# Sparse attention with normalised queries, logits and extreme from one tensor_tensor_reduce, and token factors brought to channels by matmul with identity

## The chip, the cores and the metric

The kernel runs on one core of one Trainium2 chip. The core has TensorE (PE in the profile, its weight loads PEld), VectorE (DVE), ScalarE (ACT), GpSimd (POOL) and SyncE (SP), which issues most DMAs here. The metric is the device time of one execution in microseconds; lower is better.

## The reference, cut to what matters

One layer feeds a normalised input of 1024 tokens into five parallel branches (A, B, C, D, M), whose outputs are merged by gates and projected. The change is in branch C, sparse attention with 8 heads of 64 channels and one shared key and value head:

```python
q = rms_norm(q.reshape(Bsz, L, DSA_HEADS, DSA_HD), q_norm_g)
k = rms_norm(k, k_norm_g)
...
_, sel = lax.top_k(s_idx, top_k)
...
logits = jnp.einsum('bthd,btkd->bhtk', qb, k_sel).astype(f32) * DSA_HD ** -0.5
logits = logits - slopes[None, :, None, None] * dist[:, None]
logits = jnp.where(valid[:, None], logits, -jnp.inf)
p = jax.nn.softmax(logits, axis=-1).astype(v.dtype)
return jnp.einsum('bhtk,btkd->bthd', p, v_sel)
...
out * jax.nn.silu(gate)
```

`slopes` of head h is 2 to the power of -(h + 1). The kernel does not gather: it takes the logits of all keys up to the token's own tile, and a distance of 1e30 stands for a key that was not selected.

## The kernel before, in words

The kernel is written tile by tile. A planner at build time follows the source, allocates the buffers of each tag (`tag`, `bufs`) and fixes the order of every engine's queue: what stands earlier in the source goes first, later work that is ready fills the time that the planner's own clock shows as free, and `tc.issue_after(mark)` keeps work behind a marked instruction of the same engine. On the chip every queue then runs in that order.

Before branch C runs, `sc[j]` (128 tokens of tile j by 128(j+1) keys) holds, for each token and key, the distance to the key if it is selected and 1e30 otherwise. `keys_c` (L814) normalises the keys, puts them into two stacked operands `khh` and `kll`, and leaves the values by token in `vtok`. Both gains and the factor 64 ** -0.5 are in the keys.

Branch C works on 4 blocks b of two heads (`hf` 0 and 1, 64 channels each, on the two halves of the partitions). `prep(b)` (L840) loads the raw queries `cq` by channel, transposes them on TensorE (`pq`) to get the mean square of each token and head (`ms`), and has GpSimd raise it to the power of -0.5 (`rq`). The stacks `qst` are made from the raw queries by `stacks` (L312): a rounded copy on ScalarE, the remainder `qstl` on VectorE, and a DMA that puts the remainder on the other 64 partitions. `cf` is the slope divided by the token's query factor. The gate `sg` is loaded into the same buffer as the queries.

`attend(b, j)` (L862) handles 128 tokens against 128(j+1) keys, in three steps. In step one, TensorE makes the logits in PSUM (`lg`, at most 512 columns at a time, so j above 3 takes two pieces), VectorE subtracts `cf` times the distance, and takes the maximum of the row. ScalarE takes the exponential with `rq` as its scale and adds up the row in `sm`. VectorE inverts the sum, and GpSimd multiplies the identity by it into `dg`. In step two TensorE transposes the probabilities (`pT`), and ScalarE copies them to `pt`. In step three TensorE multiplies ones by `dg`, which spreads each token's factor over 64 channels, multiplies `vtok` by `pt`, and VectorE multiplies both products into the gate `sg`. `skew` starts a new unit in each round, and runs step two of the unit before and step three of the one before that. `prep(b + 1)` stands in front of unit 4 of block b.

The tiles of `sps` (logits, transposes, outputs and spreads) share 5 PSUM banks. Around the branch lie the merges, which project each finished branch: 16 groups of 12 matmuls of 128x512 (`proj`, in 3 banks of their own), each followed by a VectorE operation (`tgl`) and an addition on GpSimd (`mg`):

```python
branch("c", branch_c)
ckx.close()
merge(2, [None] * 2 + evenly(span["c"], 28))
merge(3)
```

Behind merge 3, `prep_out` loads the output weights (`wr`) and splits them on ScalarE and VectorE. They use the space that the score tiles `sc` leave.

Of the kernel before, what the change touches and what calls it, by code (L numbers as in the profile page):

```python
# [7 lines left out]
F32 = mybir.dt.float32  # L8
F32R = mybir.dt.float32r
I32 = mybir.dt.int32  # L10
AF = mybir.ActivationFunctionType
OP = mybir.AluOpType
AX = mybir.AxisListType
PSUM = bass.MemoryType.PSUM

P = 128
D = 1024
L = 1024
NT = L // P
# [6 lines left out]
MARK = -3.0e38  # L26
# [29 lines left out]
def mixer_body(ctx, tc, a, out):  # L56
    nc = tc.nc
    S, G = nc.scalar, nc.gpsimd
    V, T = Traced(nc.vector), Traced(nc.tensor)
# [17 lines left out]
    def sps(name):  # L77
        return gps(name, "s")
# [4 lines left out]
    ident = cst.tile([P, P], F32, name="ident")  # L83
    make_identity(nc, ident)
    nhalf = cst.tile([P, 64], F32, name="nhalf")
# [51 lines left out]
    HV = (slice(0, 512), slice(512, 1024))  # L137
# [66 lines left out]
    HF = (slice(0, 4), slice(4, 8))  # L204

    def r3(t, c=P):
        return t.rearrange("p (n c) -> p n c", c=c)
# [104 lines left out]
    def stacks(pool, ps, name, bufs, eng=V):  # L312

        t = [pool.tile([P, L], F32R, name=name, tag=name, bufs=bufs) for _ in range(2)]
        lo = pool.tile([P, L], F32R, name=name + "l", tag=name + "l", bufs=1)
        halves = ((slice(0, 64), slice(64, 128)), (slice(64, 128), slice(0, 64)))
        for hv, p in zip(HV, ps):
            for i, (r, o) in enumerate(halves):
                S.activation(t[i][r, hv], p[r], AF.Copy)
                eng.tensor_tensor(lo[r, hv], p[r], t[i][r, hv].bitcast(F32), OP.subtract)  # L320
        for i, (r, o) in enumerate(halves):
            nc.sync.dma_start(t[i][o].bitcast(F32), lo[r].bitcast(F32))
        return t

    def cuts(w):

        n = -(-w // 512)
        at = [-(-w * i // (n * P)) * P for i in range(n + 1)]
        return [(at[i], at[i + 1] - at[i]) for i in range(n)]

    def scores(name, q, j, kh, kl, c0, n):

        ps = sps(name)
        qj = q[:, j * P:(j + 1) * P]
        T.matmul(ps[:, :n], qj, kh[:, c0:c0 + n], start=True, stop=False)
        T.matmul(ps[:, :n], qj, kl[:, c0:c0 + n], start=False, stop=True)
        return ps
# [190 lines left out]
    def loaded(pool, nm, b, tag, bufs):  # L528

        t = pool.tile([P, L], F32, name=tag, tag=tag, bufs=bufs)  # L530
        nc.sync.dma_start(t, zd[nm][b])
        return t

    def halves(t):
        return [t[:, hv] for hv in HV]
# [280 lines left out]
    def keys_c(gp):  # L816
        kvr = loaded(gp, "c_k", 0, "uu", 2)
        kn2 = gp.tile([P, NT, 2, 64], F32, name="kn2", tag="uu", bufs=2)
        ksq = gp.tile([P, NT, 64], F32, name="ksq", tag="mx", bufs=2)
        kss = gp.tile([P, NT], F32, name="kss")  # L820
        kps = []
        for hf in HF:
            ps = tr4("kvT", lambda i: kvr[:, (hf.start + i) * P:(hf.start + i + 1) * P])
            kps.append(ps)
            S.activation(vtok[:, hf], r3(ps)[:, :, 64:128], AF.Copy)
            S.activation(ksq[:, hf], r3(ps)[:, :, 0:64], AF.Square)
        V.reduce_sum(kss, ksq, AX.X)
        rsqrt_into(kss, kss, NT, 1.0 / 64, EPS)
        for hf, ps in zip(HF, kps):
            V.tensor_tensor(ksq[:, hf], r3(ps)[:, :, 0:64], b3(kss[:, hf], 4, 64), OP.mult)  # L830
        for i in range(2):
            V.tensor_tensor(kn2[:, :, i, :], ksq, kgain[:, None, :].to_broadcast([P, NT, 64]), OP.mult)
        for hf in HF:
            ps = tr4("knT", lambda i: kn2[:, hf.start + i].rearrange("p r c -> p (r c)"))
            c = slice(hf.start * P, hf.stop * P)
            S.activation(khh[:, c], ps, AF.Copy)
            V.tensor_tensor(kll[:, c], ps, khh[:, c].bitcast(F32), OP.subtract)

    def branch_c(gp):
        def prep(b):  # L840
            pin = halves(loaded(gp, "c_q", b, "cq", 1))
            ms = gp.tile([P, 64], F32, name="ms", tag="ms", bufs=2)[:, 0:16]
            for hf, pin1 in zip(HF, pin):
                pq = tr4("pq", lambda i: pin1[:, i * P:(i + 1) * P])
                q2 = gp.tile([P, 8, 64], F32, name="q2", tag="q2", bufs=1)
                S.activation(flat(q2), pq, AF.Square)
                V.reduce_sum(ms[:, 2 * hf.start:2 * hf.stop], q2, AX.X)
            th = stacks(gp, pin, "qst", 4)
            rq = gp.tile([P, 16], F32, name="rq", tag="rq", bufs=2)
            nrq = gp.tile([P, 16], F32, name="nrq", tag="nrq", bufs=2)  # L850
            cf = gp.tile([P, NT, 2], F32, name="cf", tag="cf", bufs=2)
            V.tensor_scalar(ms, ms, 1.0 / 64, EPS, OP.mult, OP.add)
            G.tensor_tensor(rq, ms, nhalf[:, 0:16], OP.pow)
            G.tensor_tensor(ms, ms, rq, OP.mult)
            for hf in range(2):
                G.tensor_scalar(cf[:, :, hf], r3(ms, 2)[:, :, hf], -(2.0 ** -(2 * b + hf + 1)), None, OP.mult)  # L856
            sg = silu2(gp, halves(loaded(gp, "c_gate", b, "cq", 1)), "sg")
            G.tensor_scalar(nrq, rq, -1.0, None, OP.mult)
            return th, rq, nrq, cf, sg

        def attend(b, j, th, rq, nrq, cf, sg):
            W = P * (j + 1)  # L862
            lgs = []
            mx = gp.tile([P, 2], F32, name="mx", tag="mx", bufs=4)
            sm = gp.tile([P, 2], F32, name="sm", tag="sm", bufs=4)
            dg = gp.tile([P, 2, P], F32, name="dg", tag="dg", bufs=3)
            two = slice(2 * j, 2 * j + 2)
            for hf in range(2):
                lg = gp.tile([P, L], F32, name="lg", tag="lg", bufs=4)
                for c0, n in cuts(W):  # L870
                    ps = scores("lg", th[hf], j, khh, kll, c0, n)
                    V.scalar_tensor_tensor(lg[:, c0:c0 + n], sc[j][:, c0:c0 + n], cf[:, j, hf:hf + 1], ps[:, :n], OP.mult, OP.add)
                V.reduce_max(mx[:, hf:hf + 1], lg[:, :W], AX.X)
                lgs.append(lg)
            V.tensor_tensor(mx, mx, nrq[:, two], OP.mult)
            for hf, lg in enumerate(lgs):
                S.activation(lg[:, :W], lg[:, :W], AF.Exp, scale=rq[:, 2 * j + hf:2 * j + hf + 1], bias=mx[:, hf:hf + 1], accum_out=sm[:, hf:hf + 1])  # L877
            V.reciprocal(sm, sm)
            for hf in range(2):
                G.tensor_scalar(dg[:, hf, :], ident, sm[:, hf:hf + 1], 0.5, OP.mult, OP.mult)  # L880
            yield
            pts = [gp.tile([P, L], F32, name="pt", tag="pt", bufs=3) for _ in range(2)]
            for hf, pt in enumerate(pts):
                for i0 in range(0, j + 1, 4):
                    n = min(4, j + 1 - i0)
                    ps = sps("pT")
                    for i in range(n):
                        T.transpose(ps[:, i * P:(i + 1) * P], lgs[hf][:, (i0 + i) * P:(i0 + i + 1) * P], ident)
                    S.activation(pt[:, i0 * P:(i0 + n) * P], ps[:, :n * P], AF.Copy)
            yield  # L890
            po = sps("po")
            for hf in range(2):
                T.matmul(po[64 * hf:64 * hf + 64, P:2 * P], ones[:, 0:64], dg[:, hf, :], start=True, stop=True)
            for i in range(j + 1):
                for hf in range(2):
                    T.matmul(po[64 * hf:64 * hf + 64, 0:P], vtok[:, i, :], pts[hf][:, i * P:(i + 1) * P], start=(i == 0), stop=(i == j))
            sj = sg[:, j * P:(j + 1) * P]
            V.tensor_tensor(sj, po[:, P:2 * P], sj, OP.mult)
            V.tensor_tensor(sj, po[:, 0:P], sj, OP.mult)

        nxt = prep(0)
        def units():
            nonlocal nxt
            for b in range(4):
                cur = nxt
                for j in range(NT):
                    if j == 4 and b < 3:
                        nxt = prep(b + 1)
                    yield attend(b, j, *cur)
                    if j == NT - 1:  # L910
                        last.append((b, cur[4]))
        last = []
        skew(units())
        for b, sg in last:
            nc.sync.dma_start(yd[2][b], sg)
# [463 lines left out]
```

## Time and profile before

| | |
|---|---|
| median of 3 runs | 1991.66 us (1991.17 to 1996.2) |
| the profiled execution's own time | 1991.76 us |
| its span, from first to last instruction | 1989.8 us |
| mean granted clock of TensorE | 0.986 of 2.4 GHz |
| TensorE busy in the span | 1885.3 us (95%) |
| VectorE busy | 1533.0 us (77%) |
| ScalarE busy | 780.9 us (39%) |
| GpSimd busy | 545.6 us (27%) |

The profile shows one execution. Busy time is the time in which an engine has an instruction under way; TensorE's matmuls overlap, so a group's busy time can exceed the time that it takes. Line 50 is a helper through which all VectorE and TensorE instructions pass, so groups are told apart by the names of their tiles (output <- inputs).

### The profile page before, as it was taken

The numbers are of one execution on the slowest core, as the hardware profiler recorded it, in microseconds if no ns is written. First come the engines' busy times: TensorE is split into PE (matmuls) and PEld (weight loads), VectorE is DVE, ScalarE is ACT, GpSimd is POOL, SyncE is SP. The second block draws the span as 40 slices with busy tenths as digits, with TensorE's granted clock in tenths as the row PEclk, the third lists the DMA queues.
The fourth block names the chain that finished last, engine by engine and source line by source line (L and its number), as shares of the span: only waits on it lengthen the run. The fifth ranks groups of instructions, "written<-read, shape, count | busy, mean of one in ns | idle before, by whom it ended". The sixth has DMA issues, their size and how long they took to land.

```text
span 1989.8 us, 30429 instructions
## 1 busy us (share of the span) xinstructions
PE 1885.3 (95%) x11116; PEld 1486.7 (75%) x11116; DVE 1533.0 (77%) x2699; ACT 780.9 (39%) x1511; POOL 545.6 (27%) x513
## 2 busy tenths in 40 slices
PE   6999999999999999969999999999989989999888
PEld 5777757676667787758888888888867667887767
DVE  7678958686846899798777787777787758897874
ACT  6465332323223341334222233343333737764231
POOL 5102202020200313443222222222115254444134
PEclk9999999999999999979999999999999999999999
DMA  6413102020202221233333333333368363324533
GB/s 191 116 48 70 44 17 59 17 60 17 61 31 69 53 55 48 85 100 117 106 106 117 111 111 108 109 113 112 108 219 288 126 188 104 97 86 139 170 110 132
DMA packets 187910, 199.89 MB, mean 100 GB/s; under 512 B 23641, under 2 KB 139214, under 8 KB 187762
## 3 DMA queue, kind: packets, MB, share of 16 engines
q1 hardware_dynamic: 187186, 196.91, 32.1%
q8 instruction: 88, 1.44, 0.3%
q10 hardware_dynamic: 576, 1.05, 0.1%
q14 instruction: 60, 0.49, 0.1%
HBM read 141.67 MB, written 52.05 MB: 97 GB/s over the span
## 4 chain that ended last, share of the span: by engine, by line
PE 68%; DVE 12%; issue 4%; DMA 3%; POOL 2%; ACT 2%; SPq 0%; POOLq 0%; DVEq 0%; ACTq 0%
PE pm L50 30%; PE gin L50 12%; PE proj L50 6%; PE po L50 4%; PE gate L50 2%; PE lg L50 2%; PE pT L50 2%; DVE cacc L50 1%; PE pu L50 1%; PE pst L50 1%; PE t L50 1%; DMA yr<-yd 1%; PE t2y L50 1%; DVE sc L50 1%; DVE m L50 1%
## 5 line engine op out<-in xcount | busy, mean ns | idle before, releaser
L50 PE MATMUL proj<-part,whi 128*128 128x512 f32 x640 | 210.6, 404 | 8.2 <-DVE tgl L50 3.1
L50 DVE MAX8 m<-sc 128x8 f32<-128x384 f32 (+5 forms) x192 | 170.4, 888 | 1.6
L50 DVE MATCH_REPLACE8 sc<-m,sc 128x384 f32<-128x384 f32 (+5 forms) x192 | 168.1, 876 | 0.0
L105 ACT ACTIVATE fh<-fs 128x512 fp32r<-128x512 f32 x132 | 83.1, 632 | 193.6 <-PE pm L50 187.8
L50 PEld LDWEIGHTS proj<-part,whi 128*128 128x128 f32 x640 | 121.1, 192 | 34.9 <-DVE tgl L50 4.6
L50 PE MATMUL proj<-part,wlo 128*128 128x512 f32 x320 | 128.8, 403 | 4.8 <-DVE wlo L50 4.8
L50 DVE SCALAR_TENSOR_TENSOR u<-pm,u 128x512 f32<-128x512 f32 x128 | 85.0, 684 | 47.5 <-PE pm L50 47.2
L105 ACT ACTIVATE whi<-wraw 128x512 fp32r<-128x512 f32 x106 | 66.4, 629 | 138.3 <-PE gin L50 88.9
L105 ACT ACTIVATE fh<-gr 128x512 fp32r<-128x512 f32 x90 | 56.8, 632 | 146.4 <-PE pm L50 115.3
L50 DVE TENSOR_TENSOR fl<-fs,fh 128x512 fp32r<-128x512 f32 x132 | 93.8, 713 | 3.5 <-ACT fh L105 3.5
L1154 POOL TENSOR_TENSOR fs<-gr 128x512 f32<-128x512 f32 x30 | 38.9, 1297 | 184.7 <-DVE fl L50 182.2
L1300 POOL TENSOR_TENSOR mg<-mg,tgl 128x512 f32<-128x512 f32 x48 | 67.9, 1417 | 57.4 <-DVE tgl L50 51.0
L50 DVE TENSOR_TENSOR fl<-gr,fh 128x512 fp32r<-128x512 f32 x90 | 64.1, 713 | 24.5 <-ACT fh L105 24.5
L50 DVE SCALAR_TENSOR_TENSOR cacc<-craw,pc,cacc 128x1023 f32<-128x1023 f32 (+2 forms) x60 | 77.6, 1294 | 6.3 <-ACT cacc L543 5.9
L50 DVE TENSOR_TENSOR wlo<-wraw,whi 128x512 fp32r<-128x512 f32 x82 | 59.6, 731 | 29.4 <-ACT whi L105 19.5
L50 DVE SCALAR_TENSOR_TENSOR st<-st,cda,pst 128x128 f32<-128x128 f32 x60 | 20.8, 347 | 74.4 <-PE pst L50 74.3
L50 PEld LDWEIGHTS proj<-part,wlo 128*128 128x128 f32 x320 | 61.2, 191 | 17.1 <-DVE wlo L50 5.2
L1153 POOL TENSOR_TENSOR fs<-gr 128x512 f32<-128x512 f32 x30 | 39.5, 1317 | 117.3 <-issue 117.3
L877 ACT ACTIVATE lg<-lg,mx,rq 128x128 f32<-128x128 f32 (+7 forms) x64 | 54.9, 861 | 18.5 <-DVE mx L50 16.3
L50 DVE SCALAR_TENSOR_TENSOR lg<-sc,cf,lg 128x384 f32<-128x384 f32 (+3 forms) x96 | 56.3, 605 | 6.9 <-POOL cf L856 3.8
L50 PE MATMUL pm<-h00h,fl 128*128 128x512 f32 x120 | 47.8, 398 | 12.4 <-DVE fl L50 12.4
L50 DVE SCALAR_TENSOR_TENSOR sc<-rl,iwt,sc 128x512 f32<-128x512 f32 (+3 forms) x84 | 47.1, 615 | 13.1 <-ACT rl L463 11.8
(579 smaller groups left out, 5714.1 us busy)
## 6 DMA issues: line engine op xcount, KB each, us to landing
tgl<-gd SPq DMA_DIRECT2D x80, 256.0 KB, 3.0
wraw<-in_w_in_dram SPq DMA_DIRECT2D x66, 256.0 KB, 2.9
gr<-in_w_gate_dram SPq DMA_DIRECT2D x32, 512.0 KB, 3.6
gr<-in_w_in_dram SPq DMA_DIRECT2D x28, 512.0 KB, 3.8
yr<-yd SPq DMA_DIRECT2D x40, 256.0 KB, 3.8
wraw<-in_w_branch_dram SPq DMA_DIRECT2D x40, 256.0 KB, 3.9
yd<-sg SPq DMA_DIRECT2D x16, 512.0 KB, 3.1
gd<-u SPq DMA_DIRECT2D x30, 256.0 KB, 3.8
```

Of the source, the lines that this page charges most:

```text
L50: r = f(*args, **kw)
L105: S.activation(hi, raw, AF.Copy)
L877: S.activation(lg[:, :W], lg[:, :W], AF.Exp, scale=rq[:, 2 * j + hf:2 * j + hf + 1], bias=mx[:, hf:hf + 1], accum_out=sm[:, hf:hf + 1])
L1153: eng.tensor_tensor(s3, a11, a21, OP.subtract)
L1154: eng.tensor_tensor(s1, a21, a22, OP.add)
L1300: (G if n < 4 else V).tensor_tensor(m, m, t, OP.add)
```

## The change

The values are halved in `keys_c`. In `prep`, the inverse root mean square `ms` of each token and head is brought to channels by `spread`, which multiplies a column of `ms`, read as 64 equal columns, by the identity. VectorE multiplies it and a slope (the negative of two to the power of the head's number) into the queries, and the stacks are made from these. In `attend`, one tensor_tensor_reduce for each piece adds the distance to the logits, scales by the head's factor and gives the row's minimum, which the second piece takes up from the first; the exponential is taken of the negative. The sums of a block are kept in one tile. After every fourth tile, VectorE inverts the sums of four tiles, `spread` brings them to channels, and one product of 512 columns applies them. The multiplication by `dg` goes.

```diff
-            S.activation(vtok[:, hf], r3(ps)[:, :, 64:128], AF.Copy)
+            S.activation(vtok[:, hf], r3(ps)[:, :, 64:128], AF.Copy, scale=0.5)
...
+        def spread(ps, col):
+            for i in range(4):
+                for hf in range(2):
+                    T.matmul(ps[64 * hf:64 * hf + 64, i * P:(i + 1) * P], col(i)[:, hf:hf + 1].to_broadcast([P, 64]), ident, start=True, stop=True)
+            return ps
...
         def prep(b):
-            pin = halves(loaded(gp, "c_q", b, "cq", 1))
+            q = loaded(gp, "c_q", b, "cq", 1)
...
-            th = stacks(gp, pin, "qst", 4)
-            rq = gp.tile([P, 16], F32, name="rq", tag="rq", bufs=2)
-            nrq = gp.tile([P, 16], F32, name="nrq", tag="nrq", bufs=2)
-            cf = gp.tile([P, NT, 2], F32, name="cf", tag="cf", bufs=2)
             V.tensor_scalar(ms, ms, 1.0 / 64, EPS, OP.mult, OP.add)
-            G.tensor_tensor(rq, ms, nhalf[:, 0:16], OP.pow)
-            G.tensor_tensor(ms, ms, rq, OP.mult)
-            for hf in range(2):
-                G.tensor_scalar(cf[:, :, hf], r3(ms, 2)[:, :, hf], -(2.0 ** -(2 * b + hf + 1)), None, OP.mult)
+            G.tensor_tensor(ms, ms, nhalf[:, 0:16], OP.pow)
+            for hf, hv in zip(HF, HV):
+                ps = spread(sps("rqb"), lambda i: ms[:, 2 * (hf.start + i):2 * (hf.start + i) + 2])
+                V.scalar_tensor_tensor(q[:, hv], ps, slopes[:, b:b + 1], q[:, hv], OP.mult, OP.mult)
+            th = stacks(gp, halves(q), "qst", 4)
+            sm = gp.tile([P, 16], F32, name="sm", tag="sm", bufs=2)
             sg = silu2(gp, halves(loaded(gp, "c_gate", b, "cq", 1)), "sg")
-            G.tensor_scalar(nrq, rq, -1.0, None, OP.mult)
...
-                for c0, n in cuts(W):
-                    ps = scores("lg", th[hf], j, khh, kll, c0, n)
-                    V.scalar_tensor_tensor(lg[:, c0:c0 + n], sc[j][:, c0:c0 + n], cf[:, j, hf:hf + 1], ps[:, :n], OP.mult, OP.add)
-                V.reduce_max(mx[:, hf:hf + 1], lg[:, :W], AX.X)
+                for n, (c0, w) in enumerate(cuts(W)):
+                    ps = scores("lg", th[hf], j, khh, kll, c0, w)
+                    V.tensor_tensor_reduce(lg[:, c0:c0 + w], ps[:, :w], sc[j][:, c0:c0 + w], 2.0 ** -(2 * b + hf + 1),
+                                           mn[:, 2 * hf:2 * hf + 1] if n else -MARK, OP.add, OP.min, mn[:, 2 * hf + n:2 * hf + n + 1])
                 lgs.append(lg)
-            V.tensor_tensor(mx, mx, nrq[:, two], OP.mult)
             for hf, lg in enumerate(lgs):
-                S.activation(lg[:, :W], lg[:, :W], AF.Exp, scale=rq[:, 2 * j + hf:2 * j + hf + 1], bias=mx[:, hf:hf + 1], accum_out=sm[:, hf:hf + 1])
-            V.reciprocal(sm, sm)
-            for hf in range(2):
-                G.tensor_scalar(dg[:, hf, :], ident, sm[:, hf:hf + 1], 0.5, OP.mult, OP.mult)
+                S.activation(lg[:, :W], lg[:, :W], AF.Exp, scale=-1.0, bias=mn[:, 2 * hf + n:2 * hf + n + 1], accum_out=sm[:, 2 * j + hf:2 * j + hf + 1])
...
             po = sps("po")
-            for hf in range(2):
-                T.matmul(po[64 * hf:64 * hf + 64, P:2 * P], ones[:, 0:64], dg[:, hf, :], start=True, stop=True)
...
-            V.tensor_tensor(sj, po[:, P:2 * P], sj, OP.mult)
             V.tensor_tensor(sj, po[:, 0:P], sj, OP.mult)
+            if j % 4 == 3:
+                rs = gp.tile([P, 8], F32, name="rs", tag="rs", bufs=2)
+                V.reciprocal(rs, sm[:, 2 * j - 6:2 * j + 2])
+                ps = spread(sps("rsb"), lambda i: rs[:, 2 * i:2 * i + 2])
+                s4 = sg[:, (j - 3) * P:(j + 1) * P]
+                V.tensor_tensor(s4, ps, s4, OP.mult)
+
+        slopes = gp.tile([P, 16], F32, name="slopes")
+        for b in range(4):
+            for hf in range(2):
+                G.memset(slopes[64 * hf:64 * hf + 64, b:b + 1], -2.0 ** (2 * b + hf + 1))
```

## Rows read from the trace of the kernel before

**Rows 1.** Busy time of each engine by stretch (from:to, length, busy).
```profile
core 0: us, PE busy (x) PEld busy (x) DVE busy (x) ACT busy (x) POOL busy (x), PEclk, DMA share, GB/s
1621.00:1640.00 19.00, 10.48 (x42) 8.38 (x41) 11.92 (x22) 7.23 (x16) 11.61 (x12) 0.82 0.63 198
1640.00:1812.00 172.00, 170.90 (x1414) 141.09 (x1413) 148.84 (x332) 118.64 (x258) 69.52 (x105) 0.99 0.30 92
1812.00:1830.00 18.00, 18.00 (x81) 14.88 (x80) 15.96 (x18) 5.99 (x10) 11.02 (x7) 1.00 0.59 184
1830.00:1870.00 40.00, 32.17 (x131) 25.07 (x130) 37.77 (x50) 15.21 (x26) 12.99 (x8) 0.96 0.59 187
```

**Rows 2.** Waits from 1812 to 1905 us (total, times, longest).
```profile
PE proj L50 <- DVE wlo L50: 4.8, 1, 4.8
```

**Rows 3.** TensorE's timeline in the branch (start, us, form, records).
```profile
1680.03 0.44 PE L50 MATMUL po<-dg,ones 128*64 128x128 f32 x4
1680.30 1.70 PE L50 MATMUL po<-pt,vtok 128*64 128x128 f32 x28
1681.92 0.39 PE L50 MATMUL lg<-khh,qst 128*128 128x256 f32 x1
...
1688.65 0.40 PE L50 MATMUL lg<-kll,qst 128*128 128x512 f32 x1
1688.88 0.39 PE L50 MATMUL lg<-khh,qst 128*128 128x512 f32 x1
```

**Rows 4.** TensorE's timeline near 86 us: two matmuls with broadcast weights.
```profile
86.52 0.61 PE L50 MATMUL last<-cs,ident 128*128 128x128 f32 x4
```

**Rows 5.** VectorE's groups, 1600 to 1815 us (busy, mean ns, idle before).
```profile
L50 DVE SCALAR_TENSOR_TENSOR lg<-sc,cf,lg 128x384 f32<-128x384 f32 (+3 forms) x96 | 56.3, 605 | 6.9 <-POOL cf L856 3.8 <-PE lg L50 2.7
L50 DVE TENSOR_REDUCE mx<-lg 128x1 f32<-128x128 f32 (+7 forms) x64 | 47.2, 741 | 0.1
L50 DVE TENSOR_TENSOR sg<-po,sg 128x128 f32<-128x128 f32 x64 | 18.2, 284 | 11.7 <-PE po L50 11.4
L50 DVE TENSOR_TENSOR mx<-mx,nrq 128x2 f32<-128x2 f32 x32 | 8.7, 273 | 0.1
L50 DVE RECIPROCAL sm<-sm 128x2 f32<-128x2 f32 x32 | 5.1, 160 | 5.2 <-ACT lg L877 4.9
```

**Rows 6.** Timeline of the second block's preparation, one row of each engine.
```profile
1647.95 1.09 PE L50 MATMUL pq<-ident,cq 128*128 128x128 f32 x8
...
1650.96 0.58 ACT L846 ACTIVATE q<-pq 128x512 f32<-128x512 f32 x1
...
1652.30 0.66 DVE L50 TENSOR_REDUCE ms<-q 128x8 f32<-128x512 f32 x1
...
1653.65 2.93 POOL L853 TENSOR_TENSOR rq<-ms,nhalf 128x16 f32<-128x16 f32 x1 [0.39 <-DVE ms L50]
```

**Rows 7.** VectorE's scan near 82 us, groups by form.
```profile
L50 DVE TENSOR_TENSOR_SCAN rows<-rm,ldT 16x512 f32<-16x512 f32 x2 | 2.3, 1192 | 0.0
```

**Rows 8.** GpSimd's group of dg, 1640 to 1812 us.
```profile
L880 POOL TENSOR_SCALAR dg<-ident,sm 128x128 f32<-128x128 f32 x64 | 24.2, 392 | 73.3 <-DVE sm L50 60.8 <-PE pT L50 5.6 <-PE proj L50 3.5
```

**Rows 9.** Timelines of VectorE, GpSimd and ScalarE before the first unit.
```profile
1604.20 2.12 DVE L50 TENSOR_TENSOR qstl<-cq,qst 64x512 fp32r<-64x512 f32 x3 [2.26 <-ACT qst L319]
...
1630.95 2.91 POOL L853 TENSOR_TENSOR rq<-ms,nhalf 128x16 f32<-128x16 f32 x1 [2.16 <-DVE ms L50]
...
1634.64 0.60 DVE L50 SCALAR_TENSOR_TENSOR lg<-sc,cf,lg 128x128 f32<-128x128 f32 x2 [3.77 <-POOL cf L856]
...
1637.39 0.49 ACT L877 ACTIVATE lg<-lg,mx,rq 128x128 f32<-128x128 f32 x1 [4.88 <-DVE mx L50]
```

**Rows 10.** TensorE's timeline at the branch's start.
```profile
1620.22 1.04 PE L50 MATMUL pq<-ident,cq 128*128 128x128 f32 x8
...
1638.03 0.48 PE L50 MATMUL pT<-ident,lg 128*128 128x128 f32 x1 [5.44 <-DVE lg L50]
```

**Rows 11.** DMA of the stacks' lower half, from issue to landing.
```profile
DMA to landing us min/median/max: 2.9/3.1/3.3
```

More of the change, by code (lines that the diff above doesn't have):

```diff
@@ L839, in branch_c @@
     def branch_c(gp):
+        def spread(ps, col):
[3 more added lines that the diff above has]
+            return ps
         def prep(b):
-            pin = halves(loaded(gp, "c_q", b, "cq", 1))
-            ms = gp.tile([P, 64], F32, name="ms", tag="ms", bufs=2)[:, 0:16]
-            for hf, pin1 in zip(HF, pin):
+            q = loaded(gp, "c_q", b, "cq", 1)
+            ms = gp.tile([P, 56], F32, name="ms", tag="ms", bufs=2)[:, 0:16]
+            for hf, pin1 in zip(HF, halves(q)):
                 pq = tr4("pq", lambda i: pin1[:, i * P:(i + 1) * P])
@@ L857, in prep, with attend @@
             sg = silu2(gp, halves(loaded(gp, "c_gate", b, "cq", 1)), "sg")
-            G.tensor_scalar(nrq, rq, -1.0, None, OP.mult)
-            return th, rq, nrq, cf, sg
-        def attend(b, j, th, rq, nrq, cf, sg):
+            return th, sm, sg
+        def attend(b, j, th, sm, sg):
             W = P * (j + 1)
             lgs = []
[L864 to L867, printed above, removed]
+            mn = gp.tile([P, 4], F32, name="mn", tag="mn", bufs=4)
@@ L910, in units @@
                     if j == NT - 1:
-                        last.append((b, cur[4]))
+                        last.append((b, cur[2]))
         last = []
```

## The prediction

> **What bounds the kernel now.** I looked first at the busy time of each engine by stretch. The change touches only the sparse-attention branch, which runs from about 1620 to 1812 us, and the trace divides there into three parts [rows 1]. From 1621 to 1640 TensorE is busy for 10.48 of 19 us: the first block is being prepared. From 1640 to 1812 it is busy for 170.90 of 172 us, while VectorE has 148.84, so VectorE is heavily loaded but TensorE has 1.1 us of slack. From 1830 to 1870, when the output weights are prepared, VectorE has 37.77 of 40 us and TensorE loses 7.8 us; the list of waits puts the longest of these losses on a weight split that VectorE does [rows 2].
>
> A busy TensorE need not be a full one, so I read the start times of its matmuls next [rows 3]. Two matmuls of 512 columns start 0.23 us apart (1688.65 and 1688.88), and 512 columns at 2.4 GHz are 0.213 us; the granted clock of the stretch is 0.99. There is no gap to fill. What fills it are the merge's proj matmuls, which depend on nothing in the branch and are put by the planner wherever the branch leaves TensorE free. So inside the branch a shorter dependency chain returns nothing by itself: it moves proj matmuls out of the branch to behind it. Only matmul time, and idle time of TensorE at the two edges, can move the end.
>
> **TensorE's own work.** Removed are the 64 matmuls that multiply ones by dg, in 32 pairs. The pair starts at 1680.03, and the next matmuls at 1680.30 [rows 3]: 0.27 us, together 8.6 us. Added are 16 calls of spread (two for the queries and two for the sums in each of 4 blocks), each 8 matmuls in 4 pairs, with 64 output rows each and 128 columns of identity. That is the shape of the po<-pt matmuls, of which 7 pairs (28 records) run from 1680.30 to 1681.92: 0.231 us a pair. A spread is then 0.93 us, 0.96 with the lead that the first pair shows, and 16 are 15.4 us. Weights read by broadcast have a precedent: the two full-width matmuls of `last` take 4 records from 86.52 to 86.96 [rows 4], 0.11 us a record, the rate of any other, and the 64-wide pair at 0.058 us a record shows that two halves overlap. Net **+6.8 us**; +6.2 if there is no lead, +8.6 if each pair costs 0.27.
>
> **VectorE's work.** Gone are 64 reductions (47.2 us), 32 products of mx (8.7), 32 reciprocals (5.1) and half of the 64 sg products (9.1): 70.1 us [rows 5]. Added are 16 operations of 512 elements (about 0.7 us each, worked out from the 0.66 of a reduction of that size [rows 6]) and 8 small reciprocals: 12.5 us. The 96 scalar_tensor_tensor become 96 tensor_tensor_reduce. The trace has none of these; below, they cost what they replace (56.3 us); each may also carry a small write of its extreme, and the small reciprocal's 0.16 us bounds that at 15 us for 96; above stands the only operation here that carries a value along a row, the scan, with 1192 ns for 512 elements [rows 7]. The 96 cover 36,864 columns, so 2.33 ns a column make 86 us, +30. I take +10, nearer the operation it replaces, because nothing else in its operands changes. VectorE is relieved of about 48 us (28 to 58), GpSimd of the 24.2 us of dg [rows 8]. Between 1640 and 1812 that relief is worth at most the 1.1 us that TensorE idles: I take -0.5.
>
> [...]
>
> **The first block's preparation.** Before, the query stacks are made from the raw queries, early: VectorE's split is at 1604.20, under the proj matmuls of the merge before [rows 9]. The power of the mean squares is needed only by VectorE, from 1634.64. After, the stacks need normalised queries, so the chain is serial: transposes at 1620.22 [rows 10], squares, sums, power until 1633.9 [rows 9], two spreads and two products until 1636.5, VectorE's four splits of 0.7 us until 1639.1, the transfer of the lower half, 3.1 us from issue to landing [rows 11] and about 0.4 of issue, until 1642.5. The logits, one reduce (about 0.3, as the two of [rows 9] at 1634.64) and one exponential (0.49) follow, against two of each with reductions before, so the first transposition of probabilities comes at about 1643.6 instead of 1638.03 [rows 10]: 5.6 us later. Of these TensorE uses 1.9 for spreads already counted, and perhaps 2.7 for one more proj group (12 matmuls of 0.23). Idle grows by 1.0 to 3.7 us. The granted clock is 0.82 in this stretch [rows 1], so matmuls after the pause run at 1.2 GHz for some microseconds already; a longer pause may add up to 2. I take **+3 us** (1 to 6).
>
> **The three later preparations.** The logits of unit 4 are issued behind the preparation on TensorE: before, behind the 8 transposes only. In every stretch I read, TensorE takes the matmuls that share the small PSUM banks in source order, so now the spread stands in front of unit 4's logits, unit 3's transposes and unit 2's output. It waits for squares, two sums and the power: in block 1 the transposes start at 1647.95 and end at about 1649.0, the second square is at 1650.96, its sum at 1652.30, and the power runs from 1653.65 to 1656.6 [rows 6]. That is 7.5 us, three times. Proj groups can cover it if the planner has placed them there; what it didn't foresee is lost. I take 1.5 us uncovered each, **+4.5** (0 to 22), since the 1.1 us of idle in 172 says that the planner covers waits well, while a power of 2.93 us for 16 elements is a row that it can easily price too low. The gate tile, which shares the query's buffer, is loaded later too, but is needed only by the output of unit 0; four units lie between.
>
> **The tail.** With 48 us less on VectorE the branch's units follow each other more closely, more proj matmuls are left behind the branch, and TensorE has something to do while VectorE prepares output weights. That can return the 7.8 us of 1830 to 1870 [rows 1]. The three stalls and the later start work against it by delaying the release of the score tiles, into whose space these weights are loaded. I take **-6** (0 to -7.8).
>
> **Sum.** 6.8 + 3 + 4.5 - 6 - 0.5 = +7.8. The profiled execution took 1991.76 us (span 1989.8 and 2.0 around it), 0.1 from the median of 1991.66, so 1999.5 us.
>
> **Rivals.**
> *All is absorbed.* The stalls are covered and the tail is returned in full: 6.2 + 1.0 - 7.8 = -0.6, with a branch that ends no later: 1986 to 1995 us, near 1991. For it: 1.1 us of idle in 172. Against it: the serial start. [...]
>
> *VectorE was the true bound: faster.* The planner may space the units by VectorE, whose 148.84 of 172 us [rows 1] leave it little room once its waits for TensorE are in. If closer units also let the start be filled, all idle of the three stretches (8.5 + 1.1 + 7.8 = 17.4) comes back against 6.8 of new matmuls: -10.6, 1981 us. It decides once more than 12.8 us of idle is returned; the serial start speaks against it.
>
> *The power isn't covered.* Each of three preparations stalls TensorE for 5 us, the clock falls after it (2 us together), the branch ends later and the tail returns nothing: 6.8 + 4 + 15 + 2 = +28 at the worst, 2012 to 2020 us. For it: TensorE waited 5.44 us behind VectorE in the one case before where logits depended on the power [rows 10].
>
> **How the numbers follow.** This kernel tells a change from none at about 0.3%, 6 us. The forecast, between +3 and +14, has 0.48, of which 0.12 lies under 6 us; all absorbed has 0.25; faster has 0.14; uncovered has 0.13. Slower is 0.36 + 0.13 = 0.49, the same 0.12 + 0.25 = 0.37, faster 0.14. The range is 1984 to 2012: it leaves out a good half of the faster case and half of the uncovered one. The forecast's own range is 1995 to 2006.
>
> **What would show it.** TensorE should have spread pairs of 0.23 us; tensor_tensor_reduce should lie near 0.6 us on average; the first transposition of probabilities should come about 6 us after 1638; TensorE should wait for the query spread three more times; VectorE's busy time should fall by about 48 us; idle from the branch's end to the first output product should shrink. I am wrong if the spreads start without a wait, if the first block starts as early as before, or if the idle in the tail stays.

## The result, and the profile after

The kernel takes 2018.51 us (median of 4 runs, 2016.37 to 2019.35) against 1992.29 for the kernel before on the same chip: a ratio of 1.0126, 95% interval 1.0109 to 1.0144. That is 26.2 us slower, 19 us above the predicted 1999.5 and above the range. The profiled execution has a span of 2016.7 us, 26.9 more than before.

The windows of the profile after, as in [rows 1] (from:to, length, then busy time of PE, PEld, DVE, ACT, POOL, granted clock, DMA):

```profile
1621.00:1642.00 21.00, 13.59 (x78) 10.96 (x76) 13.30 (x17) 5.84 (x10) 10.88 (x7) 0.84 0.56 157
1642.00:1814.00 172.00, 157.26 (x1406) 132.96 (x1407) 96.00 (x285) 107.48 (x255) 25.16 (x16) 0.95 0.22 67
1814.00:1850.00 36.00, 33.72 (x145) 26.60 (x144) 27.50 (x35) 12.84 (x22) 21.08 (x15) 1.00 0.67 210
1850.00:1890.00 40.00, 35.66 (x144) 27.47 (x143) 38.33 (x43) 14.55 (x25) 19.75 (x13) 0.96 0.63 192
```

The stretch of 172 us was full before (170.90, clock 0.99). Now TensorE is busy for 157.26, at a clock of 0.95, although VectorE has fallen from 148.84 to 96.00 and GpSimd from 69.52 to 25.16. Every helper is freer, and TensorE waits more. In the tail 2.28 + 4.34 = 6.6 us of idle time stay, where 7.8 were.

The list of TensorE's waits from 1600 to 1900 us (total, times, longest) names one cause:

```profile
PE rqb L50 <- POOL ms L856: 20.0, 4, 6.8
PE proj L50 <- DVE tgl L50: 6.5, 8, 2.0
PE lg L50 <- DMA qst<-qstl: 1.5, 2, 0.8
```

L856 is the power on GpSimd, rqb the spread of the queries. TensorE's timeline shows the four waits, and what follows them:

```profile
1632.24 3.68 PE L50 MATMUL rqb<-ident,ms 128*64 128x128 f32 x32 [6.83 <-POOL ms L856]
...
1642.12 0.30 PE L50 MATMUL lg<-khh,qst 128*128 128x128 f32 x1 [0.70 <-DMA qst<-qstl]
...
1644.07 0.27 PE L50 MATMUL pT<-ident,lg 128*128 128x128 f32 x1
...
1651.64 1.03 PE L50 MATMUL pq<-ident,cq 128*128 128x128 f32 x8
1658.25 3.68 PE L50 MATMUL rqb<-ident,ms 128*64 128x128 f32 x32 [5.57 <-POOL ms L856]
...
1671.77 1.04 PE L50 MATMUL rsb<-ident,rs 128*64 128x128 f32 x16
1672.74 0.50 PE L50 MATMUL lg<-khh,qst 128*128 128x512 f32 x1
...
1705.08 3.44 PE L50 MATMUL rqb<-ident,ms 128*64 128x128 f32 x32 [4.24 <-POOL ms L856]
...
1750.44 3.68 PE L50 MATMUL rqb<-ident,ms 128*64 128x128 f32 x32 [3.36 <-POOL ms L856]
```

Three things are to be seen besides the waits. One spread of sums, at full clock, goes from 1671.77 to 1672.74: 0.97 us, as worked out. The two query spreads of a block take 3.44 to 3.68 us instead of 2 x 0.97. And in the second block nothing stands between the transposes of 1651.64 and the spread: no proj group fills the 5.57 us. The first transposition of probabilities is at 1644.07 (forecast 1643.6).

The windows of the second block's query spreads and of the spread of sums at 1671.77 give the granted clock of the two (it is the third number from the end of a row):

```profile
1658.00:1662.00 4.00, 3.75 (x33) 3.42 (x33) 0.77 (x2) 0.92 (x2) 0.20 (x1) 0.50 0.02 4
1668.00:1674.00 6.00, 6.00 (x58) 5.23 (x57) 3.71 (x12) 5.97 (x14) 0.00 (x0) 1.00 0.27 86
```

Behind the wait the granted clock is 0.50, and in a busy stretch 1.00. Logits of 256 columns start 0.21 us apart behind the wait (1662.67 and 1662.88) and 0.11 further on in the branch (1709.52 and 1709.63), 0.82 and 0.43 ns a column. Half the clock accounts for the difference between 3.68 and 2 x 0.97.

What fills those 5.57 us, on the other engines:

```profile
1652.28 0.60 ACT L853 ACTIVATE q<-pq 128x512 f32<-128x512 f32 x1 [0.66 <-PE pq L50]
...
1652.91 0.69 DVE L50 TENSOR_REDUCE ms<-q 128x8 f32<-128x512 f32 x1 [0.32 <-ACT q L853]
1654.32 0.69 DVE L50 TENSOR_REDUCE ms<-q 128x8 f32<-128x512 f32 x1 [0.72 <-ACT q L853]
1655.04 0.18 DVE L50 TENSOR_SCALAR ms<-ms 128x16 f32<-128x16 f32 x1
...
1655.29 2.90 POOL L856 TENSOR_TENSOR ms<-ms,nhalf 128x16 f32<-128x16 f32 x1 [1.37 <-DVE ms L50]
```

Each step starts when the one before it ends; half of the time is the power.

VectorE's groups from 1600 to 1815 us (count | busy, mean ns), to be laid beside [rows 5]:

```profile
L50 DVE CUSTOM_DVE_ANT_0 lg<-lg,sc 128x384 f32<-128x384 f32 (+3 forms) x64 | 34.2, 556 | 7.0 <-PE lg L50 5.9
L50 DVE CUSTOM_DVE_ANT_0 lg<-lg,sc,mn 128x384 f32<-128x384 f32 (+2 forms) x32 | 18.9, 615 | 1.6
...
L50 DVE TENSOR_TENSOR sg<-po,sg 128x128 f32<-128x128 f32 x32 | 9.3, 292 | 31.4 <-PE po L50 31.0
L50 DVE DVE_READ_ACCUMULATOR2_ANT mn<- 128x1 f32 x96 | 8.0, 83 | 0.0
L50 DVE SCALAR_TENSOR_TENSOR cq<-rqb,slopes,cq 128x512 f32<-128x512 f32 x8 | 6.0, 751 | 25.5 <-PE rqb L50 25.5
L50 DVE TENSOR_TENSOR sg<-rsb,sg 128x512 f32<-128x512 f32 x8 | 5.5, 692 | 4.3 <-PE rsb L50 4.3
```

tensor_tensor_reduce shows as CUSTOM_DVE_ANT_0 with a read of its extreme behind it: 34.2 + 18.9 + 8.0 = 61.1 us, 4.8 above the 56.3 of what it replaces. VectorE's part of the change does what it says.

### The profile page after: what moved, and what is told of

Same layout as the page of the kernel before. It is cut to its first block, busy times and chain, and to the rows that moved or that the text cites. A ratio compares the mean times of both kernels' runs of the same rounds, so it can differ in the third digit from the quotient of the medians.

```text
span 2016.7 us, 30504 instructions
## 1 busy us (share of the span) xinstructions
PE 1899.7 (94%) x11244; PEld 1501.5 (74%) x11244; DVE 1495.5 (74%) x2659; ACT 773.6 (38%) x1511; POOL 518.2 (26%) x441
## 5 line engine op out<-in xcount | busy, mean ns | idle before, releaser
L50 DVE TENSOR_TENSOR wlo<-wraw,whi 128x512 fp32r<-128x512 f32 x82 | 61.3, 752 | 30.3 <-ACT whi L105 19.7
L50 DVE SCALAR_TENSOR_TENSOR tgl<-tgl,proj 128x512 f32<-128x512 f32 x64 | 43.5, 681 | 25.3 <-PE proj L50 22.2
L50 PE MATMUL gin<-h00h,whi 128*128 128x512 f32 x132 | 54.8, 415 | 0.0
```

The costliest lines, as they stand in the source:

```text
L50: r = f(*args, **kw)
```

## The experiments

Two questions were open: what opens the four waits, and what is left of the loss without them. Between transposes and spread only proj groups can work. Theory A (supply): they are held back by marks of the merge behind the branch. Theory B (price): the order of TensorE's instructions, which is fixed when the kernel is built, leaves too small a gap for the way through the power. The rivals for the loss as a whole: the tail sets the end, or VectorE does. Times are medians, and a gain is counted from the changed kernel's 2018.51; the kernel before, run beside these, had medians of 1992.3 to 1993.2.

**1. Marks of the merge taken away.**

```diff
-    merge(2, [None] * 2 + evenly(span["c"], 28))
+    merge(2)
```

> The changed kernel, with the merge behind the branch released from its 28 marks, so that its proj groups may fill any gap of the branch. TensorE waits 20.0 us in all for the four query spreads (6.83, 5.57, 4.24 and 3.36). Theory A (supply): the gap stays open because no proj group is released yet; in the second block none stood between transposes and spread. Then the wait of the second block falls from 5.57 to about 2.5, the first by up to 2, and the time by 3 to 7 us, to about 2013. Theory B (price): the gap is left too small because the planner takes the way through squares, sums and power to be shorter than it is, however many groups it has. Then 2 to 4 us of wait stay before each spread, and the time falls by less than 3 us.

2014.14 us, ratio 1.0103 (1.0084 to 1.0122): 4.4 us back. Eleven proj records now stand in the second block's gap, and its wait goes from 5.57 to 4.07 us; all four together go from 20.0 to 18.5. In the fourth block the spreads also run at full clock behind a wait of 3.92 us (1.97 instead of 3.68). So A is true for one block, which still waits for 4.07 us instead of the 2.5 that A expected, and explains a small part.

**2. No power.**

```diff
-            G.tensor_tensor(ms, ms, nhalf[:, 0:16], OP.pow)
```

> The changed kernel without the power on GpSimd: the spread takes the mean squares themselves, so the queries are not normalised as the reference wants. The power lasts 2.90 us. If its length is what the planner misses (theory B), the four waits fall from 20.0 to about 8 us, the slow clock behind them shrinks, and the time falls by 12 to 16 us, to about 2004. If the planner had its full length in its books, it leaves 3 us less of a gap, the waits stay near 20 us and the time falls by less than 3 us.

1998.82 us, ratio 1.0030 (1.0021 to 1.0040): 19.7 us back from one instruction a block, more than the 12 to 16 expected. Its waits, and the second block's spread:

```profile
PE rqb L50 <- DVE ms L50: 6.8, 3, 3.7
```
```profile
1645.57 1.03 PE L50 MATMUL pq<-ident,cq 128*128 128x128 f32 x8
1649.29 1.97 PE L50 MATMUL rqb<-ident,ms 128*64 128x128 f32 x32 [2.68 <-DVE ms L50]
```

The waits fall by 13.2 us, 3.3 for each block on average: the 2.9 of the power and its hand-over. With them most of the slow clock goes: the spreads of the three later blocks take 1.97 us, the first block's 3.17. In the order of TensorE's instructions the gaps between transposes and spread hold 14, 0, 17 and 19 proj matmuls with the power, and 13, 0, 16 and 17 without. Taking the power out shrank the gaps by 0 to 2 matmuls of 0.23 us, at most half a microsecond. That is what the order had set aside for an instruction of 2.90 us. Such gaps would also stay short if no more proj matmuls had been ready, whatever the price. The changed kernel's timeline speaks against that, here at the last block:

```profile
1746.47 0.61 PE L50 MATMUL proj<-part,whi 128*128 128x512 f32 x2
1750.44 3.68 PE L50 MATMUL rqb<-ident,ms 128*64 128x128 f32 x32 [3.36 <-POOL ms L856]
...
1756.53 0.48 PE L50 MATMUL proj<-part,wlo 128*128 128x512 f32 x1
```

Counted in twelves, the spread cuts a proj group after its 2nd matmul in the first block, after its 9th in the third and its 8th in the fourth. The rest of the group, which goes into the same bank and is held back by no further mark, follows only behind the spread. In the second block the spread falls between two groups, and there experiment 1 shows what the marks hold back. So Theory B holds for three blocks, and the price is short by almost the whole length of the power. The price itself is inferred from the orders; no run shows it directly.

**3. Idle matmuls in the gap.**

```diff
-                ps = spread(sps("rqb"), lambda i: ms[:, 2 * (hf.start + i):2 * (hf.start + i) + 2])
+                ps = sps("rqb")
+                for i in range(32 if hf.start == 0 else 0):
+                    T.matmul(ps[:, i % 4 * P:(i % 4 + 1) * P], ident, ident, start=True, stop=True)
+                spread(ps, lambda i: ms[:, 2 * (hf.start + i):2 * (hf.start + i) + 2])
```

> The changed kernel with 32 idle matmuls (identity by identity, about 0.12 us each at full clock, 3.9 us) in front of each query spread, into the bank that the spread then overwrites: TensorE works instead of waiting, and nothing else is removed. If the clock that falls in the waits has a price of its own (spread at 3.4 to 3.7 us instead of 1.9, slow logits behind it), the time falls by 4 to 8 us, to about 2012, with spreads near 1.9 us. If only the waiting counts, the time stays within 2 us of 2018.5.

2025.17 us, ratio 1.0160 (1.0140 to 1.0181): 6.7 slower, where either reading had expected a gain or nothing. The timeline says why:

```profile
1657.14 7.31 PE L50 MATMUL rqb<-ident 128*128 128x128 f32 x64
1664.38 1.97 PE L50 MATMUL rqb<-ident,ms 128*64 128x128 f32 x32
```

The 32 matmuls take 7.31 us, not 3.9. Each of them left two records (x64) and took 0.23 us; 0.12 was the price of a transposition (eight of pT, from 1679.06 to 1680.03 in the kernel before). It gained nothing, but its sum can be made: 4 x 7.31 = 29.2 us of work come in and 20.0 - 3.2 = 16.8 of waiting go. Three blocks' spreads run in 1.97 us each, the first in about 2.9; against 14.5 that is 5.7 saved. 29.2 - 16.8 - 5.7 = 6.7, the difference of the medians. That it meets so exactly is luck: two of the four runs took 2022.2 us and two 2028.1, and the profile is of the slower two. In it the branch starts at 1625.96 us instead of 1621.17, and from there to the end it takes 4.9 us longer than the changed kernel. By that the lower clock behind the waits has a price of its own of some 6 to 8 us.

**4. The later preparations in two pieces.**

```diff
-                    if j == 4 and b < 3:
-                        nxt = prep(b + 1)
+                    if j == 3 and b < 3:
+                        half = prep(b + 1)
+                    if j == 5 and b < 3:
+                        nxt = prep2(b + 1, *half)
```

(prep ends behind the power; prep2 is the rest of it.)

> The changed kernel with the preparation of the next block in two pieces: transposes, squares, sums and power at unit 3, spread, products and stacks at unit 5. Stall theory: the three later waits (5.57 + 4.24 + 3.36 = 13.2 us) and some 5 us of slow clock go, the first (6.83) stays, and the time falls by 13 to 18 us, to about 2003. Rival (the tail): what the branch gives back is lost behind it, since output weights and VectorE set the end; then idle time grows in the 80 us behind the branch and the time falls by less than 5 us.

2009.21 us, ratio 1.0082 (1.0067 to 1.0097): 9.3 back, between the two forecasts. The three later waits are 0, 1.24 and 1.23 us, and the spreads take 1.97; by that 10.7 + 4.9 us are saved. But TensorE now idles for 7.24 us from 1814 to 1850, where it was 2.28 (and for 1.11 from 1850 to 1890, where it was 4.34), and for 2.0 more behind a query load that comes too late for unit 3; the first wait is 7.34 instead of 6.83, and this profile's branch starts 1.1 us later. The stall is real, and part of what it gives back is lost in small pieces, in the tail and ahead of it.

**5. Scalar_tensor_tensor and a reduction in place of tensor_tensor_reduce.**

```diff
-                    V.tensor_tensor_reduce(lg[:, c0:c0 + w], ps[:, :w], sc[j][:, c0:c0 + w], 2.0 ** -(2 * b + hf + 1),
-                                           mn[:, 2 * hf:2 * hf + 1] if n else -MARK, OP.add, OP.min, mn[:, 2 * hf + n:2 * hf + n + 1])
+                    V.scalar_tensor_tensor(lg[:, c0:c0 + w], sc[j][:, c0:c0 + w], 2.0 ** -(2 * b + hf + 1), ps[:, :w], OP.mult, OP.add)
+                V.tensor_reduce(mn[:, 2 * hf + n:2 * hf + n + 1], lg[:, :W], axis=AX.X, op=OP.min)
...
-                G.memset(slopes[64 * hf:64 * hf + 64, b:b + 1], -2.0 ** (2 * b + hf + 1))
+                G.memset(slopes[64 * hf:64 * hf + 64, b:b + 1], -1.0)
```

> The changed kernel with its 96 tensor_tensor_reduce and their reads (61.1 us) replaced by 96 scalar_tensor_tensor and 64 reductions (56.3 + 47.2 in the kernel before): VectorE gets about 42 us more, TensorE nothing. If TensorE and its waits set the time, the four waits for the spread stay at 17 to 21 us, the added VectorE time is filled with proj groups and the time stays between 2013 and 2024. Rival (VectorE's relief counts): it rises by 15 us or more, to 2034 and beyond.

2017.33 us, ratio 1.0122 (1.0109 to 1.0135). VectorE's busy time in the 172 us rises from 96.00 to 128.31, and the time doesn't move: the waits for the spread are 20.5. What tensor_tensor_reduce saves is worth nothing in this kernel.

**6. The sums alone, on the kernel before.**

```diff
-            V.reciprocal(sm, sm)
-            for hf in range(2):
-                G.tensor_scalar(dg[:, hf, :], ident, sm[:, hf:hf + 1], 0.5, OP.mult, OP.mult)
...
-                T.matmul(po[64 * hf:64 * hf + 64, P:2 * P], ones[:, 0:64], dg[:, hf, :], start=True, stop=True)
...
+            if j % 4 == 3:
+                rs = gp.tile([P, 8], F32, name="rs", tag="rs", bufs=2)
+                V.reciprocal(rs, sm[:, 2 * j - 6:2 * j + 2])
+                ps = spread(sps("rsb"), lambda i: rs[:, 2 * i:2 * i + 2])
+                s4 = sg[:, (j - 3) * P:(j + 1) * P]
+                V.tensor_tensor(s4, ps, s4, OP.mult)
```

> The kernel before with one part of the change alone: the reciprocals of the sums for four units at a time, brought to the channels by the spread, in place of dg and its matmuls; queries, logits and extremes as before. TensorE loses 8.6 us of dg matmuls and gets 8 spreads of 0.96, -0.9; VectorE loses 32 small reciprocals and 24 products net, about -8. No new wait is expected. Theory: 1988 to 1993, the same as before. Rival (the tail gives back what VectorE is spared): 1983 to 1987.

1999.63 us (12 runs), ratio 1.0027 (1.0017 to 1.0037): slower, against both forecasts. There is no wait for the spread of sums on TensorE. The profiled execution reaches the first block's transposes at 1624.77 us instead of 1620.22 [rows 10], although no engine's instruction order differs before that point. That part belongs to the execution: the same matmuls ran at a lower clock, for instance at 0.83 from 1460 to 1480 us, where the kernel before shows 1.00. From the transposes to the end it takes 5.2 us more. 2.8 of them are idle time of TensorE, in small waits of the branch and the tail; why they come was not settled. At any rate this half of the change is no gain.

**7. All powers early.** As in 4, at units 4 and 6, and the first block's piece ahead of the merge in front of the branch:

```diff
-        nxt = prep(0)
+        half = prep(0)
+        merge(1, [None] * 4 + evenly(span["m"], 12))
+        topk([(share[nm], vspan[nm]) for nm in share])
+        nxt = prep2(0, *half)
```

> The changed kernel with every power started early: the first block's transposes, squares and power are issued ahead of the merge in front of the branch, the later ones at unit 4, and spread, products and stacks follow at unit 6. Stall theory: of 20.0 us of waits for the spread less than 3 stay, the spreads run at 1.9 us instead of 3.4 to 3.7, and the time falls by 20 to 27 us, to between 1991 and 1999. Rival (the tail): the branch ends earlier but the time stays above 2003, with the idle time of TensorE behind the branch grown by 8 us or more.

2001.91 us, ratio 1.0047 (1.0034 to 1.0060): 16.6 back. No wait for the spread is left, and the spreads take 1.92 to 1.97 us. The branch ends 30 us earlier, with its last po at 1782.53 instead of 1812.68, by the waits, by the clock and by 25 proj matmuls that have left it (75 lie between its first logits and its end, not 100); 474 instead of 440 come behind it. Some of the gain goes into a wait of 4.7 us of the first logits for the stacks' transfer and into 7.4 us of idle time from 1814 to 1850. The gain is less than the 20 to 27 us of the stall theory, and the kernel is still 9.6 us slower than before, with no wait for a spread left to blame.

**8. A cheaper spread, on 7.**

```diff
-        def spread(ps, col):
-            for i in range(4):
-                for hf in range(2):
-                    T.matmul(ps[64 * hf:64 * hf + 64, i * P:(i + 1) * P], col(i)[:, hf:hf + 1].to_broadcast([P, 64]), ident, start=True, stop=True)
-            return ps
+        def spread(name, cols):
+            w = gp.tile([P, 8, 64], F32, name="w", tag="w", bufs=1)
+            S.activation(w, b3(cols, 8, 64), AF.Copy)
+            return tr4(name, lambda i: flat(w[:, 2 * i:2 * i + 2]))
```

> As the kernel with every power started early (median 2001.91), but the spread made of transposes: ScalarE writes the eight columns 64 times each into a tile of 128x512, and TensorE transposes it in 4 instructions of 0.12 us instead of 8 matmuls in pairs of 0.23, so a spread takes 0.48 us instead of 0.96 and the 16 of them 7.7 instead of 15.4. If TensorE's added matmuls are what is left of the loss, the time falls by 6 to 9 us, to about 1994. Rival (what is left is idle time behind the branch): it stays within 3 us of 2001.9.

1994.12 us, ratio 1.0005 (0.9996 to 1.0015): 7.8 us less than experiment 7, and level with the kernel before. That this meets the 7.7 worked out is partly luck: from 1800 to 1850 us the granted clock is 0.93 in the profile of 7 and 1.00 in that of 8, for about the same 40 us of matmuls, which is worth some 3 us by itself (an estimate from these numbers). TensorE's groups of the spreads, from 1600 to 1800 us, in 7 and then in 8:

```profile
L50 PE MATMUL rsb<-ident,rs 128*64 128x128 f32 x128 | 9.1, 273 | 0.0
L50 PE MATMUL rqb<-ident,ms 128*64 128x128 f32 x128 | 7.7, 273 | 0.0
```
```profile
L50 PE MATMUL rsb<-ident,w 128*128 128x128 f32 x32 | 5.2, 286 | 0.0
L50 PE MATMUL rqb<-ident,w 128*128 128x128 f32 x32 | 5.0, 279 | 2.1 <-ACT w L842 2.1
```

**9 and 10. Output weights spread over the last merges**, on 8 and on the kernel before:

```diff
+            wx2 = ExitStack()
+            wx2.enter_context(tc.issue_after(v3[len(v3) * (0 + k) // 5]))
             for n, x in ((0, r[0, 0]), (1, r[1, 0])):
...
+            wx2.close()
...
+    v30 = len(V.log)
     merge(3)
...
-        prep_out()
         merge(4, (), V)
+        v3 = V.log[v30:]
+        prep_out()
```

(The first lines stand in prep_out's loop over its four passes k. The edit does two things: merge 4 now stands ahead of the output weights in the source, and the passes are held behind marks.)

> The kernel with early powers and transposed spreads (median 1994.12), with the preparation of the output weights spread over the two last merges: its four passes are held behind marks in VectorE's order of these merges. In that kernel TensorE idles for 12 us between 1800 and 1850, mostly behind VectorE's tgl, which stands in line with the weight splits. If the spared VectorE time is lost because the splits crowd there, the wait for tgl falls from 9.5 to 4 us or less and the time by 4 to 7 us, to 1987 to 1990, faster than before. Rival (the splits only move): the same idle time shows up in front of the output products and the time stays within 2 us of 1994.

> The same spacing of the output weights in the kernel before the change. There VectorE is 86% busy in the branch, and TensorE idles 7.8 us between 1830 and 1870. If the spacing works for itself, this gains as much, 4 to 7 us, to about 1987, and the version with early powers has no merit of its own; if it needs the branch to end early, the time stays within 2 us of 1992.5.

On 8: 1989.17 us, ratio 0.9981 (0.9971 to 0.9990). On the kernel before: 1986.13 us, ratio 0.9963 (0.9951 to 0.9976), the fastest of all. Both beat both kernels. The windows from 1800 to 1850 us, of 8 and then of 9 (the idle time of 8 is 9.5 us there, not the 12 of the expectation):

```profile
1800.00:1850.00 50.00, 40.47 (x167) 29.93 (x165) 47.36 (x54) 16.77 (x29) 27.26 (x17) 1.00 0.62 194
```
```profile
1800.00:1850.00 50.00, 45.46 (x194) 35.53 (x193) 34.22 (x42) 15.68 (x27) 28.02 (x20) 1.00 0.65 203
```

VectorE's 47.36 us fall to 34.22 and TensorE's idle time from 9.5 to 4.5; the wait for tgl goes from 9.5 to 4.0. But the kernel before gains 6.2 us by the same edit, so the edit works for itself, and the change contributes nothing to it even with its stalls cured. Whether the marks or the place of merge 4 does it, no run tells apart.

## Why the prediction was wrong

The rival that it gave 0.13, "the power isn't covered", is what happened, near its upper end. That rival's total came out better than its terms: it had too much for the first block and too little for the clock. Step by step:

**The three later preparations** is the step that failed. It put 1.5 us uncovered on each, 4.5 in all, and had named the reason to take more: a power of 2.93 us "that it can easily price too low". It measured 5.57 + 4.24 + 3.36 = 13.2, well inside the stated bound of 22. The choice leaned on 1.1 us of idle time in 172, but that row tells how well the planner covers what it prices rightly. In the kernel before no instruction of TensorE behind the first block waited for the power, so the row said nothing about it; [rows 10] had the only case that did, with 5.44 us of wait. Experiment 2 shows the mechanism.

**The clock** behind those three waits had a place in the rival alone (2 us together). The spreads took 3.68, 3.44 and 3.68 us there, against 1.97 at full clock in experiment 2. With the logits that follow them, TensorE worked for 14.0 us at a clock of 0.50 behind the three waits, which at half speed cost 7.0. So these preparations cost 13.2 + 7.0 = 20.2 us instead of 4.5: 15.7 of the 19 us that the forecast was off.

**TensorE's own work** was right in its unit price, 0.97 us a spread. Experiments 7 and 8 show that the added matmuls aren't free: with cheaper spreads the kernel was 7.8 us faster. They don't show the 6.8 by itself, since the clock moved too.

**VectorE** was right in size, and worth as little as the step said. The groups of the change's own operations fall by 52.0 us (48 forecast); tensor_tensor_reduce cost +4.8, not +10. The operation itself took (34.2 + 18.9) / 96 = 0.55 us, below the 0.59 of the 96 scalar_tensor_tensor. The excess is the separate read of 0.083. "VectorE was the true bound" is refuted by experiment 5.

**The first block** came as late as forecast, but did not cost the 3 us. Its idle time did not grow: 6.83 + 1.5 us, where 5.4 [rows 10] and 3.1 for the first block's squares stood before. Nor did the slow clock, which the kernel before already had behind its own two waits:

```profile
1626.20:1629.60 3.40, 3.40 (x10) 2.66 (x9) 2.51 (x4) 0.77 (x2) 1.36 (x2) 0.50 0.89 280
1636.50:1643.30 6.80, 5.27 (x16) 4.46 (x17) 5.40 (x16) 2.90 (x10) 3.13 (x6) 0.50 0.36 118
```

That is 8.7 us of work at a clock of 0.50, and in the changed kernel 4.3 in this block. At half speed that gives back 2.2 us, so this step was about 5 us too high and hid part of the miss.

**The tail** returned about 1 us, not 6: 6.6 us of idle time for 7.8. That "the idle in the tail stays" was one of the prediction's own signs of being wrong. Its longest wait before, the 4.8 us of [rows 2], was for a split of weights of the last merge, not of output weights; both stand in VectorE's queue. Less work for VectorE in the branch does not thin out these splits behind it; experiments 9 and 10 show that their order does.

**The balance** of the two profiles: the first block's transposes start 0.95 us later (1621.17 for 1620.22). From there to the end TensorE idles for 40.3 us instead of 28.8, +11.5; the clock in the branch costs +4.8 (18.3 us of work at 0.50, where 8.7 were); the matmuls +6.8. That is 24.1 of 26.9; the other 2.8 are busy time that was not put down to any one step.

## What to carry to other kernels

Before a matmul is made to depend on a short chain through other engines, find the row of the chain's slowest instruction and ask whether the order that covers waits knows its length; idle time that is small today says nothing about a wait that doesn't exist yet. Where such a chain can't be shortened, issue its long instruction a unit or two ahead of its use. And on a kernel whose TensorE is full, weigh a change by TensorE's own microseconds first: here VectorE was spared 52 us and GpSimd its 24 us of dg, and no run shows a gain from either.

## What the runs showed that was not expected

- The length of the last wait did not by itself tell the clock behind it: the two spreads of a block ran in 1.97 us behind waits of 3.92 (experiment 1), 2.68 (experiment 2) and 1.24 us (experiment 4), but in 3.68 behind one of 3.36 (the changed kernel).
- Work ahead of the branch, in the same order on TensorE, ended at different times: the last output matmul of the branch before began between 1588.72 us (experiment 2) and 1595.74 (experiment 3) in the profiles, 1589.84 in the kernel before. A good part of that belongs to the execution and not to the program: the four runs of experiment 3 are of one program, and the two of 2022.2 us had a mean granted clock of 0.988, the two of 2028.1 had 0.985 and 0.986. It limits what one profile can say about a few microseconds.
- ScalarE's exponential of 128 columns took 0.40 us with a constant scale (1642.90 in the changed kernel) and 0.49 [rows 9] with one scale per partition.
